# Where the gate products of the heads stand in an attention stage, and one gate step between two kinds of turning

## The chip, the cores and the metric

The kernel runs on one core of a Trainium2 chip. The metric is the time of one execution on the device, in microseconds (us); the kernel before takes 645.65 us, the median of three runs (645.23 to 645.66). One execution was also recorded by the hardware profiler. Names of engines as in the profile: PE is TensorE (matmuls and transposes), PEld its weight loads, ACT ScalarE, DVE VectorE, POOL GpSimd, SP the engine that issues most DMAs. L152 is line 152 of the kernel before; behind line 688 the changed kernel's lines are three higher.

## The reference

One layer of an encoder: attention heads and a gated linear recurrence (LRU) side by side, on 512 tokens of 2048 numbers each.

```python
h = rms_norm(x, norm_w)
proj = jnp.einsum('bsd,de->bse', h, w_in)
q, k, v, g_attn, xr, g_lru = jnp.split(proj, SPLITS, axis=-1)
attn_out = attention_group(q, k, v, q_norm_w, k_norm_w)
lru_out = lru_group(xr, conv_w, conv_b, lru_wa, ...)
mixed = jnp.concatenate([rms_norm(attn_out, attn_norm_w) * jax.nn.silu(g_attn),
                         rms_norm(lru_out, lru_norm_w) * jax.nn.silu(g_lru)], axis=-1)
return x + jnp.einsum('bse,ed->bsd', mixed, w_out)
```

There are 8 query heads and 2 key/value heads of 128; all queries of a head see all 512 keys. `g_attn` and `g_lru` are 1024 columns wide each.

## The kernel before

Every product of fp32 values is made of three matmuls (`mm3`, L152 to L154): both operands are split into a rounded high part and a remainder (`wh`, `wl` of a weight; L224 on ACT rounds, L226 on DVE subtracts), and high by high, high by low and low by high are added up in one PSUM bank. The stages follow each other on PE: the LRU input, keys and values, queries, then **the attention stage** (some 255 to 418 us in the profile), which alone the change touches, then the rest of the gates and the output projection.

In the attention stage two streams are woven on PE by hand; PE's and POOL's order is the program's, while ACT's, DVE's and SP's is set by a scheduler from priorities, ahead of the run, and each engine then works strictly through its own list.

**The chain** is `attention` (from L671). It runs over half heads d = 0 to 18; half head d makes the scores of two of the four 128-query blocks of head d//2, and what earlier half heads left to do. Within a half head the order on PE is: `values` (even d only: 12 matmuls of head (d-4)//2); `turn_weights` twice, the transposes (L639) of two probability blocks of half head d-2, split on ACT and DVE at L581 and L582; at odd d up to 11 `turned`, the transposes (L577) of the queries of head d//2 + 2, split by the same lines; then the two scores S0 and S1 (three matmuls each). Each score is reduced on DVE (L626), scaled on ACT (L627) and exponentiated on ACT (L630, one [128 x 512] pass that is the last to read the bank), its sum inverted on DVE (L631) and the block scaled on POOL (L632).

Everything the chain writes on PE goes to four PSUM banks named `mm` in turn, so the instruction after four others waits until the oldest bank has been read.

**The fill** is `gates` (from L1256), a list of steps. Each step is six [128 x 128] by [128 x 512] matmuls. `weave` takes as many steps from it as the chain yields: four before half head 0, then `STEPS = 1, 3`, one behind S0 and three behind S1. `PLAN` (L1254) is the list of units; a unit is two steps.

- `u` (`gl_units`, L1165): the LRU gate, a [512 x 2048] by [2048 x 1024] product done as **seven products** of half the size in each dimension (named P1, Q6, P2, Q5, Q3, Q7, Q4 in that order; eight steps each), with sums and differences of quarters. All seven accumulate in the same two `pj` banks (first half of the tokens, second half). After the last step of a product `product_done` (L1140) empties the two banks on ACT (P1, L1147) or DVE (L1150 to L1161). The left operand of P1, P2 and Q4 is x itself, that of the others is a sum read back from DRAM and split at L1180 and L1181 (`dh`, `dl`).
- `G` (`ga_units`, L1197): a chunk of the gate of heads 0 and 1, 256 input columns of the eight, accumulating over all eight chunks in the other two `pj` banks. One [128 x 512] tile holds a chunk's weights, split at L1208 and L1209.
- `H`: the same for heads 2 and 3, after the others.

Weights arrive through three raw buffers (`wr`), loaded from SP, and four pairs of `wh`, `wl`. At every second step from the fifth on, POOL issues one DMA that builds sums of `w_out` in DRAM (L835, L838).

Of the kernel before, what the change touches and what calls it, by code (L numbers as in the profile page):

```python
# [23 lines left out]
NH = 8  # L24
# [19 lines left out]
STEPS = 1, 3  # L44
# [18 lines left out]
def hybrid_kernel(  # L63
# [540 lines left out]
    def turned(rot, h, by=SOON):  # L604

        q = b4(F32R)
        soon(split_ps, turn(rot, h), q[:, 0, :], q[:, 1, :], by=by)
        return q[:, 0, :], q[:, 1, :]

    def weights(q, g, t, r, by):  # L610

        qh, ql = q
        tt = slice(t * P, (t + 1) * P)
        sc = mm()
        mm3(sc, qh[:, tt], ql[:, tt], kth[g], ktl[g], True, True)
        return soon(softmax, sc, r, by=by)
# [18 lines left out]
    def turn_weights(p, t, pth, ptl):  # L635
        tt = slice(t * P, (t + 1) * P)
        pt = mm()
        for s in range(NT):
            nc.tensor.transpose(pt[:, s * P : (s + 1) * P], p[:, s * P : (s + 1) * P], ident)  # L639
        p3 = pt.rearrange("p (s q) -> p s q", q=P)  # L640
        soon(split_ps, p3, pth[:, :, tt], ptl[:, :, tt])

    def values(h, pth, ptl):

        gs = slice(h // G * HD, (h // G + 1) * HD)
        o = mm()
        for s in range(NT):
            mm3(o, vh[s][:, gs], vl[s][:, gs], pth[:, s, :], ptl[:, s, :], s == 0, s == NT - 1)
        if h % 2 == 0:
            ap_[h // 2] = aring.tile([P, 2, SEQ], F32, name=nm("av"))  # L650
        av, asum = ap_[h // 2][:, h % 2, :], sums["a"]
        nc.scalar.copy(av, o)
        if h == 0:
            nc.scalar.activation(asum, av, AF.Square)
        else:
            sq = k2()
            nc.scalar.activation(sq, av, AF.Square)
            nc.gpsimd.tensor_add(asum, asum, sq)

    def turned_weights():  # L660
        return [
            pools["low"].tile([P, NT, SEQ], F32R, tag="pt", bufs=ATT_PT, name=nm("pt"))
            for _ in range(2)
        ]
# [6 lines left out]
    def attention(rots):  # L671

        pts, ps_ = {0: turned_weights()}, {}
        qs = {h: turned(rots[0], h, FIRST) for h in range(2)}
        yield 4
        for d in range(2 * NH + 3):
            h, half = divmod(d - 4, 2)
            if h >= 0 and half == 0:
                values(h, *pts.pop(h))
            h, half = divmod(d - 2, 2)  # L680
            if 0 <= h < NH:
                if half == 0:
                    pts[h] = pts.get(h) or turned_weights()
                for t in (2 * half, 2 * half + 1):
                    turn_weights(ps_.pop((h, t)), t, *pts[h])
            h, half = divmod(d, 2)
            if h < NH:
                if half == 1 and h + 2 < NH:
                    qs[h + 2] = turned(rots[(h + 2) // G], (h + 2) % G)
                for e, t in enumerate((2 * half, 2 * half + 1)):  # L690
                    r = q_r[NT * (h // G) + t][:, h % G : h % G + 1]
                    ps_[h, t] = weights(qs[h], h // G, t, r, SOON if d else FIRST)
                    yield STEPS[e]
            elif d < 2 * NH + 2:
                yield 2
            else:
                yield 0
# [360 lines left out]
    for step in proj_feat(C_XR, a1, first, given):  # L1058
# [8 lines left out]
        c, e = step  # L1067
# [153 lines left out]
    def lru_gates(j):  # L1221

        tiles = [halves_of[n, s] for n in (("c", "d"), ("b", "a"))[j] for s in range(2)]
        for t, tile_ in enumerate(tiles):
            nc.scalar.activation(tile_, tile_, AF.Silu, scale=rstd[:, t : t + 1])
        yield
        for t, tile_ in enumerate(tiles):
            nc.scalar.activation(tile_, tile_, AF.Identity, scale=r_lru[0][:, t : t + 1])
        yield
        for m in range(4):  # L1230
            pt = mm()
            for t, tile_ in enumerate(tiles):
                nc.tensor.transpose(  # L1233
                    pt[:, t * P : (t + 1) * P], tile_[:, m * P : (m + 1) * P], ident
                )
            dst = hp[2 * j + m // 2][:, m % 2, :]
            nc.vector.scalar_tensor_tensor(
                dst, dst, v1(R_LN + 4 * j + m), pt, op0=ALU.mult, op1=ALU.mult
            )
            yield  # L1240

    def heads_gates(res):

        for g in res:
            nc.scalar.activation(g, g, AF.Silu)
        yield
        for e, g in enumerate(res):
            dst = ap_[0][:, e, :]
            nc.vector.scalar_tensor_tensor(
                dst, dst, v1(R_AN + e), g, op0=ALU.mult, op1=ALU.mult  # L1250
            )
            yield

    PLAN = "GGGuuuu" "uuuu" "uuuuG" "uuuuG" "uuGuuG" "uuuuG" "uuuu" "HHHHHHHH"  # L1254

    def gates():  # L1256
        early, b = [], [pj() for _ in range(4)]
        units = {"u": gl_units(b[:2]), "G": ga_units(0, early, b[2:]), "H": ga_units(1, late, b[2:])}
        todo = iter(())
        for n, unit in enumerate(itertools.chain.from_iterable((u, u) for u in PLAN)):  # L1260
            done = next(units[unit])
            if n >= 4 and n % 2 == 0:
                next(out_sums, None)
            if done == "Q4":
                todo = itertools.chain(todo, lru_gates(1))
            elif unit == "G" and len(early) == 2 and n == PLAN.rindex("G") * 2 + 1:
                todo = itertools.chain(lru_gates(0), heads_gates(early))
# [5 lines left out]
    with tc.manual_schedule(engines={mybir.EngineType.Pool}):  # L1273
        weave(fill, attention(rots))
        for _ in range(8):
            next(fill)
# [107 lines left out]
```

## Time and profile before

| what | value |
|---|---|
| median of three runs | 645.65 us |
| the profiled execution | 644.75 us |
| its span, first to last instruction | 643.0 us |
| PE busy in the span | 637.2 us (99%) |
| 255 to 440 us: PE, DVE, ACT, POOL busy | 183.97, 138.91, 143.61, 69.03 of 185.00 us |
| granted clock of TensorE in that window | 1.00 |

A row of the timeline gives an instruction's start, its duration, engine, line, operation, what it writes and reads, and, in brackets, idle time ahead of it and what ended that. Matmuls overlap: a [128 x 512] one has a duration of 0.39 us while the next starts 0.23 us after it, so "busy" holds short waits too, and the distance between starts is what tells a wait.

### The profile page before, as it was taken

The page shows a single profiled execution, that of the slowest core. Times are in us where ns is not written, and L with a number is a line of the kernel's source. Part 1 is how long each engine was busy: PE and PEld are TensorE (multiplying, and loading weights), DVE is VectorE, ACT ScalarE, POOL GpSimd, SP SyncE. Part 2 cuts the span into 40 slices and gives each one's busy share as a digit, 9 for nine tenths or more (in the row PEclk, how much of TensorE's full clock was granted, in tenths as well). Part 3 has the DMA queues.
Part 4 walks back from the last instruction along what each step waited for, and adds up shares of the span by engine and source line. Part 5 has one row for each costly group of instructions (what it writes and reads, how often), then busy time and mean ns, then how long its engine had stood idle before and what let it go on. Part 6 is the DMA issues. An engine that isn't in the chain of part 4 may idle for free.

```text
span 643.0 us, 8959 instructions
## 1 busy us (share of the span) xinstructions
PE 637.2 (99%) x2962; PEld 527.6 (82%) x2962; DVE 508.3 (79%) x886; ACT 392.2 (61%) x733; POOL 132.4 (21%) x173
## 2 busy tenths in 40 slices
PE   9999999999999999999999999999999999999997
PEld 6888888888888888887888888888888888888886
DVE  5877679996699994977677868749928988699994
ACT  3543799489955524877696897764444654343441
POOL 0003303223051501543343343221000000010000
PEclk9999999999999999999999999999999999999999
DMA  8947977898767555499989977763365857586322
GB/s 294 293 140 207 234 202 161 245 240 200 171 164 226 165 178 168 148 250 269 264 219 260 266 193 193 164 162 102 98 195 192 298 178 245 186 278 213 120 93 98
DMA packets 68782, 128.19 MB, mean 199 GB/s; under 512 B 5504, under 2 KB 24320, under 8 KB 68480
## 3 DMA queue, kind: packets, MB, share of 16 engines
q1 hardware_dynamic: 55856, 90.25, 43.0%
q0 software_dynamic: 12704, 37.23, 25.5%
q8 instruction: 23, 0.38, 0.2%
q14 instruction: 23, 0.19, 0.1%
q10 hardware_dynamic: 176, 0.14, 0.1%
HBM read 119.21 MB, written 41.95 MB: 251 GB/s over the span
## 4 chain that ended last, share of the span: by engine, by line
PE 97%; DVE 1%; ACT 1%; issue 0%
PE pj L152 19%; PE pj L154 19%; PE pj L153 19%; PE mm L989 13%; PE pj L989 11%; PE mm L153 3%; PE mm L152 3%; PE mm L154 3%; PE mm L639 2%; PE mm L256 1%; PE pj L332 1%; PE mm L577 1%; PE mm L1233 1%; PE mm L1028 0%; DVE pt L582 0%; PE mm L722 0%
## 5 line engine op out<-in xcount | busy, mean ns | idle before, releaser
L224 ACT CAST wh<-wr 128x512 fp32r<-128x512 f32 x151 | 90.0, 618 | 60.8 <-PE pj L154 21.1
L226 DVE TENSOR_TENSOR wl<-wr,wh 128x512 fp32r<-128x512 f32 (+1 forms) x153 | 103.8, 701 | 23.9 <-ACT wh L224 22.4
L152 PE MATMUL pj<-x,wh 128*128 128x512 f32 x248 | 97.8, 394 | 0.0
L153 PE MATMUL pj<-x,wh 128*128 128x512 f32 x248 | 96.7, 390 | 0.0
L154 PE MATMUL pj<-x,wl 128*128 128x512 f32 x248 | 96.7, 390 | 0.0
L152 PE MATMUL pj<-wh,x 128*128 128x512 f32 x240 | 94.1, 392 | 0.6 <-DVE ev L1150 0.6
L154 PE MATMUL pj<-wh,x 128*128 128x512 f32 x240 | 93.5, 390 | 0.0
L153 PE MATMUL pj<-wl,x 128*128 128x512 f32 x240 | 93.4, 389 | 0.0
L783 ACT CAST oh<-rw 128x512 fp32r<-128x512 f32 x94 | 56.3, 620 | 38.8 <-PE mm L989 15.5
L784 DVE TENSOR_TENSOR ol<-rw,oh 128x512 fp32r<-128x512 f32 x94 | 61.7, 685 | 10.8 <-ACT oh L783 6.5
L153 PEld LDWEIGHTS pj<-x,wh 128*128 128x128 f32 x248 | 46.6, 188 | 9.8 <-DVE x L259 0.5
L154 PEld LDWEIGHTS pj<-x,wl 128*128 128x128 f32 x248 | 46.5, 188 | 9.7
L152 PEld LDWEIGHTS pj<-x,wh 128*128 128x128 f32 x248 | 46.6, 188 | 9.6
L152 PEld LDWEIGHTS pj<-wh,x 128*128 128x128 f32 x240 | 45.1, 188 | 10.1 <-DVE ev L1150 1.0
L154 PEld LDWEIGHTS pj<-wh,x 128*128 128x128 f32 x240 | 45.0, 188 | 9.5
L153 PEld LDWEIGHTS pj<-wl,x 128*128 128x128 f32 x240 | 45.1, 188 | 9.3
L989 PE MATMUL mm<-ol,mh 128*128 128x512 f32 (+1 forms) x128 | 49.0, 382 | 0.0
L989 PE MATMUL mm<-oh,ml 128*128 128x512 f32 (+1 forms) x128 | 48.9, 382 | 0.0
L989 PE MATMUL mm<-oh,mh 128*128 128x512 f32 (+1 forms) x128 | 48.9, 382 | 0.0
L921 POOL DMA_DIRECT2D out_dram<-xt x12 | 6.5, 541 | 189.5 <-DVE xt L957 139.8
L632 POOL TENSOR_SCALAR k<-k,sm 128x512 f32<-128x512 f32 x32 | 27.7, 866 | 67.7 <-DVE sm L631 56.2
L989 PE MATMUL pj<-oh,mh 128*128 128x512 f32 (+1 forms) x104 | 39.7, 382 | 0.0
(240 smaller groups left out, 1351.3 us busy)
## 6 DMA issues: line engine op xcount, KB each, us to landing
wr<-in_w_in_dram SPq DMA_DIRECT2D x59, 512.0 KB, 4.3
rw<-in_w_out_dram SPq DMA_DIRECT2D x63, 256.0 KB, 3.6
gs<-in_w_in_dram POOLq DMA_DIRECT2D x24, 512.0 KB, 6.6
ts<-in_w_out_dram POOLq DMA_DIRECT2D x24, 512.0 KB, 7.8
wr<-gs SPq DMA_DIRECT2D x16, 512.0 KB, 5.2
rw<-ts SPq DMA_DIRECT2D x31, 256.0 KB, 4.4
wr<-in_w_in_dram SPq DMA_DIRECT2D x17, 256.0 KB, 4.4
gs<-gs POOLq DMA_DIRECT2D x8, 512.0 KB, 7.3
```

Source lines behind the costliest of these rows:

```text
L152: nc.tensor.matmul(acc, lh, rh, start=start, stop=False)
L153: nc.tensor.matmul(acc, lh, rl, start=False, stop=False)
L154: nc.tensor.matmul(acc, ll, rh, start=False, stop=stop)
L224: rounded(hi[:, c], raw[:, k, c])
L226: nc.vector.tensor_sub(lo[:, c], raw[:, k, c], f(hi[:, c]))
L256: nc.tensor.transpose(pt[:, t * P : (t + 1) * P], xc[:, h * n + t, ks], ident)
L632: nc.gpsimd.tensor_scalar(p, p, sm, 0.0, op0=ALU.mult, op1=ALU.add)
L639: nc.tensor.transpose(pt[:, s * P : (s + 1) * P], p[:, s * P : (s + 1) * P], ident)
L783: nc.scalar.copy(hi, src)
L784: nc.vector.tensor_sub(lo, src, f(hi))
L921: (queue or nc.gpsimd).dma_start(of[t * P : (t + 1) * P, os_], xts[g][t][:, cs])
L989: nc.tensor.matmul(bank[key][:, to], lh[:, a, ts_], rh[:, cols], start=i == 0 and j == 0, stop=i == 7 and j == 2,)
```

## The change

Two edits, both on the order of the stage; every computation stays.

In `PLAN` the 36 units `u` and `G` are the same ones, placed otherwise. Before, three chunks `G` stood at the start, none behind P1 and Q6, one behind each of P2, Q5, Q3 and Q7, and one in the middle of Q3. Now two stand at the start and one behind each of the first six products. From the end of Q3 on the list is as before.

In `attention`, at d = 3, 5, 7, 9 and 11, one step is taken between `turn_weights` and `turned`, and one less behind S1, so that a half head still takes four.

```diff
             if h < NH:
-                if half == 1 and h + 2 < NH:
+                turn = half == 1 and h + 2 < NH
+                if turn:
+                    if d > 1:
+                        yield 1
                     qs[h + 2] = turned(rots[(h + 2) // G], (h + 2) % G)
                 for e, t in enumerate((2 * half, 2 * half + 1)):
                     r = q_r[NT * (h // G) + t][:, h % G : h % G + 1]
                     ps_[h, t] = weights(qs[h], h // G, t, r, SOON if d else FIRST)
-                    yield STEPS[e]
+                    yield STEPS[e] - (e and turn and d > 1)
...
-    PLAN = "GGGuuuu" "uuuu" "uuuuG" "uuuuG" "uuGuuG" "uuuuG" "uuuu" "HHHHHHHH"
+    PLAN = "GGuuuuG" "uuuuG" "uuuuG" "uuuuG" "uuuuG" "uuuuG" "uuuu" "HHHHHHHH"
```

Three places show how the instructions move.

PE, where P1 ends and Q6 begins (banks `pj_524`, `pj_525` are those of the seven products, `pj_526`, `pj_527` those of `G`). Before:

```order
L152 MATMUL pj_525_2637<-wh_579_2852,x2_120_526 128x512
L153 MATMUL pj_525_2637<-wl_580_2853,x2_120_526 128x512
L154 MATMUL pj_525_2637<-wh_579_2852,x2_121_527 128x512
L152 MATMUL pj_524_2636<-wh_590_2892,dh_588_2888 128x512
L153 MATMUL pj_524_2636<-wl_591_2893,dh_588_2888 128x512
L154 MATMUL pj_524_2636<-wh_590_2892,dl_589_2889 128x512
```

Now:

```order
L152 MATMUL pj_527_2639<-x2_73_305,wh_581_2856 128x512
L153 MATMUL pj_527_2639<-x2_74_306,wh_581_2856 128x512
L154 MATMUL pj_527_2639<-x2_73_305,wl_582_2857 128x512
L152 MATMUL pj_524_2636<-wh_590_2892,dh_588_2888 128x512
L153 MATMUL pj_524_2636<-wl_591_2893,dh_588_2888 128x512
L154 MATMUL pj_524_2636<-wh_590_2892,dl_589_2889 128x512
```

Directly ahead of Q6's first matmul stood P1's last; now the second of two steps of `G` stands there, and P1's last step is ahead of the half head's transposes and its two scores.

DVE in half head 9: `pt` is the split of the two turned probability blocks (it empties the banks mm_749 and mm_750 before, mm_743 and mm_744 now), the `ev` rows empty the two product banks behind Q5, `b4` is the split of turned queries. Before:

```order
L1155 TENSOR_TENSOR ev_747_3535<-pj_524_2636,ev_641_3099 128x512
L226 TENSOR_TENSOR wl_770_3616<-wr_764_3604,wh_769_3615 128x512
L1155 TENSOR_TENSOR ev_748_3537<-pj_525_2637,ev_642_3101 128x512
L1181 TENSOR_TENSOR dl_783_3681<-draw_517_2615,dh_782_3680 128x512
L226 TENSOR_TENSOR wl_785_3685<-wr_781_3677,wh_784_3684 128x512
L582 TENSOR_TENSOR pt_722_3440<-mm_749_3539,pt_721_3439 128x4x128
L582 TENSOR_TENSOR pt_722_3440<-mm_750_3546,pt_721_3439 128x4x128
L582 TENSOR_TENSOR b4_751_3553<-mm_752_3554,b4_751_3553 128x512
```

Now:

```order
L1184 TENSOR_TENSOR dl_779_3672<-draw_516_2614,dh_778_3671 128x512
L226 TENSOR_TENSOR wl_781_3676<-wr_777_3668,wh_780_3675 128x512
L582 TENSOR_TENSOR pt_718_3431<-mm_743_3526,pt_717_3430 128x4x128
L582 TENSOR_TENSOR pt_718_3431<-mm_744_3533,pt_717_3430 128x4x128
L226 TENSOR_TENSOR wl_783_3680<-wr_777_3668,wh_782_3679 128x512
L582 TENSOR_TENSOR b4_752_3562<-mm_753_3563,b4_752_3562 128x512
L1158 TENSOR_TENSOR ev_758_3588<-pj_524_2636,ev_641_3099 128x512
L1158 TENSOR_TENSOR ev_759_3590<-pj_525_2637,ev_642_3101 128x512
```

The two `pt` rows, which stood behind the emptying of Q5's banks and a pair of splits, now stand ahead of it.

ACT in half head 7: `pt` is the split of turned probabilities, `b4` that of queries, the `ev` rows are the LRU gate's Silu and scaling of a finished quarter (L1225 and L1228 before, L1228 and L1231 now), the rows with `k2` the exponentials of S0 and S1. Before, up to the exponential of S1:

```order
L1228 ACTIVATE ev_585_2881<-ev_585_2881,r_l_2365 128x512
L224 CAST wh_732_3474<-wr_729_3467 128x512
L1228 ACTIVATE ev_586_2883<-ev_586_2883,r_l_2365 128x512
L627 ACTIVATE mx_697_3345<-mx_697_3345,q_r2_94 128x1
L1180 CAST dh_730_3470<-draw_516_2614 128x512
L224 CAST wh_734_3478<-wr_729_3467 128x512
L630 ACT_TABLE_LOAD
L630 ACTIVATE k2_698_3348,sm_699_3349<-mm_696_3341,mx_697_3345,q_r2_94 128x512
...
L627 ACTIVATE mx_708_3379<-mx_708_3379,q_r3_95 128x1
L630 ACTIVATE k2_709_3382,sm_710_3383<-mm_707_3375,mx_708_3379,q_r3_95 128x512
```

Now:

```order
L1228 ACTIVATE ev_572_2824<-ev_572_2824,rstd_104 128x512
L581 CAST b4_697_3346<-mm_698_3347 128x512
L1228 ACTIVATE ev_573_2826<-ev_573_2826,rstd_104 128x512
L627 ACTIVATE mx_700_3358<-mx_700_3358,q_r2_94 128x1
L224 CAST wh_730_3469<-wr_725_3458 128x512
L630 ACT_TABLE_LOAD
L630 ACTIVATE k2_701_3361,sm_702_3362<-mm_699_3354,mx_700_3358,q_r2_94 128x512
L224 CAST wh_739_3505<-wr_736_3498 128x512
L627 ACTIVATE mx_704_3376<-mx_704_3376,q_r3_95 128x1
L1183 CAST dh_737_3501<-draw_516_2614 128x512
L224 CAST wh_741_3509<-wr_736_3498 128x512
L630 ACTIVATE k2_705_3379,sm_706_3380<-mm_703_3372,mx_704_3376,q_r3_95 128x512
```

Between the query split and the exponential of S1 there are two scalings (L1228 before) fewer; they now follow that exponential. The Silu pair and its table load (one row above those shown), of which the table load and the first Silu stood ahead of the two `pt` splits, now stand behind both.

## The prediction

> **What bounds the kernel now.** I read the page's first and fourth parts, then the wait list of PE for the stage that the change touches, then the timeline of PE at each wait, and last ACT's and DVE's timeline at the places that get less room. The page says that PE is the bound and the chain of waits is PE itself:
>
> ```profile
> PE 637.2 (99%) x2962; PEld 527.6 (82%) x2962; DVE 508.3 (79%) x886; ACT 392.2 (61%) x733; POOL 132.4 (21%) x173
> PE 97%; DVE 1%; ACT 1%; issue 0%
> ```
>
> So a change that only reorders can gain what PE waits, and nothing else: all matmuls stay. The list of PE's waits between 255 and 440 us (engine, line, waited for: us in total, times, longest) seems to leave under a microsecond:
>
> ```profile
> PE pj L152 <- DVE ev L1150: 0.6, 1, 0.6
> PE pj L152 <- ACT ev L1147: 0.2, 1, 0.2
> ```
>
> But a matmul's duration reaches 0.16 us past the start of the next, and hides that much of any wait. The starts tell it whole. PE's timeline in four places of the stage:
>
> ```profile
> 279.54 0.39 PE L154 MATMUL pj<-wh,x 128*128 128x512 f32 x1
> 280.18 0.50 PE L152 MATMUL pj<-wh,dh 128*128 128x512 f32 x1 [0.24 <-ACT ev L1147]
> 280.51 0.39 PE L153 MATMUL pj<-wl,dh 128*128 128x512 f32 x1
> ...
> 297.54 0.39 PE L152 MATMUL pj<-wh,dh 128*128 128x512 f32 x1
> ...
> 298.68 0.39 PE L154 MATMUL pj<-wh,dl 128*128 128x512 f32 x1
> 299.67 0.50 PE L152 MATMUL pj<-wh,x 128*128 128x512 f32 x1 [0.60 <-DVE ev L1150]
> 300.00 0.40 PE L153 MATMUL pj<-wl,x 128*128 128x512 f32 x1
> ...
> 342.90 0.40 PE L154 MATMUL pj<-x,wl 128*128 128x512 f32 x1
> 343.36 0.50 PE L152 MATMUL mm<-kt,b 128*128 128x512 f32 x1
> 343.69 0.40 PE L153 MATMUL mm<-kt,b 128*128 128x512 f32 x1
> ...
> 415.04 0.39 PE L152 MATMUL mm<-pt,v 128*128 128x512 f32 x1
> 415.55 0.50 PE L153 MATMUL mm<-pt,v 128*128 128x512 f32 x1
> 415.89 0.40 PE L154 MATMUL mm<-pt,v 128*128 128x512 f32 x1
> ```
>
> From 297.54 to 298.68 there are five starts: 0.228 us each, so a step of six takes 1.37. Against that, with the late start behind the wait counted too (0.33 where 0.23 is usual):
> - first matmul of Q6 (280.18): 0.64 - 0.23 = 0.41, and 0.10 behind it: **0.51**;
> - first of P2 (299.67): 0.99 - 0.23 = 0.76, and 0.10: **0.86**;
> - S1 of half head 9 (343.36): 0.46 - 0.23 = 0.23, and 0.10: **0.33**;
> - the last head's values (415.04): 0.51 - 0.23 = 0.28, and 0.11: **0.39**.
>
> I went through the starts from 255 to 440 us and found no other over 0.1 us that is not the plain change from transposes to matmuls. The four are 2.09 us: that is all the change can win.
>
> **What they wait for.** The brackets name it at 280.18 and 299.67; the chain of waits has the row ahead of 280.18, and those ahead of 343.36 (start, us, what):
>
> ```profile
> 279.65 0.48 ACT ev L1147
> ...
> 340.82 0.68 DVE ev L1155
> 341.50 0.60 DVE dl L1181
> 342.10 0.60 DVE wl L226
> 342.70 0.61 DVE pt L582
> ```
>
> At the first two it is the product banks: the next product begins directly behind the one before, and ACT or DVE has to empty the banks first. At 343.36 it is an `mm` bank: S1 takes the bank of the first turned probability block, whose split (`pt`, L582) stood in DVE's list behind the emptying of Q5's banks, a `dl` and a `wl`. The fourth (the values) lies where neither PE's nor the other engines' order changes.
>
> **The change part by part.**
>
> *A chunk of G behind P1 and behind Q6.* Two steps, 2.7 us, on the other two banks now stand between the products. From P1's last step to Q6's first there are now eight transposes (0.9 us), two scores (0.7 each) and the two steps, 5 us in all, for two copies of some 0.5 us. From Q6 to P2 it is the two steps and eight transposes, 3.6 us, for two DVE rows of 0.6 us. Both waits go: -0.51 and -0.86. The two chunks came from the start (three to two) and from the middle of Q3. At the start, P1 is now needed one unit, 2.7 us, earlier; its weights' split takes the place in ACT's and DVE's lists that the third chunk had, and SP's list loads them where it loaded that chunk. Until the end of Q3 the units stand at most one unit from where they stood, so I cost the loads at nothing: the list of PE's waits has no DMA in it. POOL's DMA issues keep their order; five of about 1 us each move ahead of one probability scaling. The latest of the scalings in the middle of the stage is that of S1 of half head 7:
>
> ```profile
> 332.96 0.69 POOL L632 TENSOR_SCALAR k<-k,sm 128x512 f32<-128x512 f32 x1 [1.36 <-DVE sm L631]
> ```
>
> It ends at 333.65, and the transposes of half head 9 that need it begin at 339.74 (below): 6.1 us. I cost this at nothing too.
>
> *One step between turned probabilities and turned queries, five times.* It gives the bank of the first block one more step before S1 takes it, and in half head 9 DVE's new list has `pt` ahead of the emptying. The turned blocks are there at 339.74 + 1.03:
>
> ```profile
> 339.74 1.03 PE L639 MATMUL mm<-ident,k 128*128 128x128 f32 x8
> 340.75 1.06 ACT L581 CAST pt<-mm 128x512 fp32r<-128x512 f32 x2
> 339.99 0.90 DVE L226 TENSOR_TENSOR wl<-wr,wh 128x512 fp32r<-128x512 f32 x1
> ```
>
> ACT has a `dh` and a `wh` in front, which wait for the step ahead of the transposes to release their buffers: 339.8 + 1.1, two casts to 342.0, DVE's splits to 342.7 (a DVE row can be stretched, 0.90 here for 0.68, while POOL works). S1 comes at 343.13 + 1.37 = 344.5. The wait goes with 1.8 us to spare: -0.33.
>
> Its price on PE is a second change between transposes and matmuls. The trace has the very pattern where gate transposes are woven in:
>
> ```profile
> 401.74 0.60 PE L1233 MATMUL mm<-ident,ev 128*128 128x128 f32 x4
> ...
> 403.56 0.60 PE L1233 MATMUL mm<-ident,ev 128*128 128x128 f32 x4
> ```
>
> Four transposes and six matmuls take 1.82 us; four at 0.109 (eight from 339.74 to the queries' at 340.61) and 1.37 make 1.80. So 0.02 each, five times: **+0.10**.
>
> *What the same step takes away.* In those half heads only two steps, not three, follow S1, so S1's bank has 1.37 us less until the next half head's S0 takes it. Before, half head 8 was nearest:
>
> ```profile
> 321.14 1.03 PE L639 MATMUL mm<-ident,k 128*128 128x128 f32 x8
> 322.58 1.06 ACT L581 CAST pt<-mm 128x512 fp32r<-128x512 f32 x2
> 324.64 0.72 ACT L1228 ACTIVATE ev<-ev,r_l 128x512 f32<-128x512 f32 x1
> 327.72 1.28 ACT L630 ACT_TABLE_LOAD   x1
> 331.73 0.78 ACT L630 ACTIVATE k<-mm,mx,q_r 128x512 f32<-128x512 f32 x1
> 332.82 0.48 PE L152 MATMUL mm<-kt,b 128*128 128x512 f32 x1
> ```
>
> The last ACT row is the exponential of S1 of half head 7: it ended at 332.51, 0.31 us ahead of S0. With the same list it would now be 1.06 late. But the list is another: from the end of the `pt` casts (323.64) to that exponential's end it took 8.87 us; two scalings leave the stretch (0.72 each with 0.1 of overlap, -1.2), two casts too (0.52 each, -1.0), a Silu and its table load enter (1.28 and 0.6, +1.9): 8.5. And the casts no longer stand behind a table load: the transposes are all done at 321.14 + 1.03, so the second cast, half of the 1.06, ends at about 322.75 rather than 323.64. That makes 331.3, some 1.5 us ahead of S0. I take no wait.
>
> The Trainium skill, page "ScalarE: Activation LUTs", section "What ACT_TABLE_LOAD costs", gives 2.66 us for a switch of tables, a load of about 1.28 and a drain of about 1.38. The load agrees with the row (1.28); a drain does not show, since the exponential of S0 starts 0.02 behind the load's end (329.00):
>
> ```profile
> 329.02 0.78 ACT L630 ACTIVATE k<-mm,mx,q_r 128x512 f32<-128x512 f32 x1
> ```
>
> By the page the two switches in the new stretch would take 2.8 us more, S0 would wait 1.3, and the sum would come out at 645.5.
>
> Half heads 12 and 13 get tighter too. In ACT's new list one `pt` cast of half head 13 (half of a 1.05 pair) stands ahead of the exponential whose bank S1 takes:
>
> ```profile
> 378.57 0.77 ACT L630 ACTIVATE k<-mm,mx,q_r 128x512 f32<-128x512 f32 x1
> 379.33 1.05 ACT L581 CAST pt<-mm 128x512 fp32r<-128x512 f32 x2
> 380.22 0.39 PE L152 MATMUL mm<-kt,b 128*128 128x512 f32 x1
> ```
>
> It ended 0.88 us before S1; less 0.53 leaves 0.35, and a `dh` cast ahead of it that now waits for its buffer may take most of that. From nothing to 0.4 us: I take **+0.10**. In half head 12 the copy of the values' bank falls behind two `pt` casts, about 1.1 us later, with 0.5 us left: 0 to 0.4, I take 0.
>
> *Sum.* -0.51 - 0.86 - 0.33 + 0.10 + 0.10 = **-1.50 us**. The profiled execution took 644.75 us, of which the span is 643.0; it would take 643.25 with a span of 641.5. That execution is 0.9 below the median shown, so the forecast for the median is 645.65 - 1.50 = **644.15 us**, 0.23% faster. About 0.2%, 1.3 us, is what a measurement of this kernel can tell from no change: the forecast lies just past that line.
>
> **The rivals.**
>
> 1. *The even half heads pay.* The cover of S1's bank is too short where ACT is late: half head 8 by 1.06 + 0.10, or half heads 12 and 13 by 0.4 each. For it: 0.31 us was all that was left in half head 8. Against it: the new ACT list above. Net -0.3 to -0.8: 644.9 to 645.3, no change that can be told. Chance 0.25, of which hardly 0.02 for a switch of tables that costs more than its row.
> 2. *The third wait stays, or another of its size comes.* The two at the product boundaries go, nothing else: -1.37 + 0.20 = -1.17, 644.5. For it: DVE is 79% busy and its order is the scheduler's. Chance 0.11.
> 3. *The fourth wait goes as well*, because ACT reaches the tail earlier: -1.9, 643.75. Against it: the lists there are row for row the same, and hang on PE. Chance 0.06.
> 4. *Slower.* The shortened cover decides in every even half head from 4 to 12: the exponential of S1 ends but 0.31 us ahead of where S0 stood, as in half head 7, and S0 now comes 1.37 earlier. Each place then costs 1.06 + 0.10 = 1.16. One is paid by the gain of 1.50 with little left, two leave 645.65 - 1.50 + 2.32 = 646.5, no change that can be told; it decides from the third, 645.65 - 1.50 + 3.48 = 647.6. Against it: that half head had the Silu and its table on ACT. Two half heads later the room was ten times that:
>
> ```profile
> 347.64 0.77 ACT L630 ACTIVATE k<-mm,mx,q_r 128x512 f32<-128x512 f32 x1
> 351.79 0.48 PE L152 MATMUL mm<-kt,b 128*128 128x512 f32 x1
> ```
>
> That is 348.41 against 351.79, 3.4 us, of which 2.0 are left. Chance 0.06.
>
> That the change might not do what it says I leave out: PE's order shows a chunk of G at each of the six boundaries.
>
> **How the numbers follow.** The forecast itself (three waits gone, at most 0.4 us of new ones, so 643.8 to 644.6) gets 0.52; rivals 1 to 4 get 0.25, 0.11, 0.06, 0.06. Faster by over 0.2% means below 644.36: some 0.44 of the forecast's 0.52, rival 3, and 0.04 of rival 2, 0.54 in all. Within 0.2%: the rest of the forecast, rival 1 and most of rival 2, 0.40. Slower: 0.06. The range goes from 643.6 (all four waits gone, or a good set of runs) to 645.3 (rival 1).
>
> **What would show it.** In the changed kernel's profile: no bracket at the first matmul of Q6 and of P2, and starts 0.23 us apart there or right behind a G step; S1 of half head 9 on time; the wait at the last values still 0.39; PE's busy time less by under a microsecond and the span near 641.5. The forecast is wrong if S0 of half head 8 or S1 of half heads 12 or 13 starts late behind an ACT row, or if the first steps of P1 at 261 us wait for weights.

## The result and the profile after

The changed kernel takes **646.56 us** (median of 22 runs, 645.62 to 647.53); the kernel before, on the same chip, 645.47 us (22 runs, 644.81 to 646.35). The ratio is 1.0017, with a 95% interval of 1.0010 to 1.0023: the change is slower by 1.1 us. The forecast was 644.15, with a range from 643.6 to 645.3, 1.50 below a median of 645.65.

The page of the changed kernel has a share of busy PE like that of before, but its chain of waits has DMA in it, where before it was 97% PE. Of these 3%, some 19 us, the weight load below is 8.99 us; another load, of 7.64 us, stands at the kernel's start (3.76 us), far ahead of the stage, and e13 below, the same kernel once more, has 1%:

```profile
PE 638.1 (99%) x2962; PEld 528.0 (82%) x2962; DVE 507.8 (79%) x886; ACT 392.8 (61%) x733; POOL 135.3 (21%) x173
PE 90%; ACT 4%; DMA 3%; DVE 1%; issue 1%; SPq 0%; ACTq 0%
```

The list of PE's waits between 255 and 440 us (line, waited for: us in total, times, longest) has lost both rows of the product banks and has three new ones:

```profile
PE mm L152 <- DVE pt L582: 1.4, 1, 1.4
PE mm L152 <- ACT k L630: 0.5, 1, 0.5
PE mm L1236 <- ACT k L630: 0.2, 1, 0.2
```

PE's timeline shows the places of the prediction: the first matmul of Q6 behind a step of `G`, the first of P2 behind transposes, S1 of half heads 9, 12 and 13, and the last values:

```profile
281.11 0.39 PE L154 MATMUL pj<-x,wl 128*128 128x512 f32 x1
281.34 0.39 PE L152 MATMUL pj<-wh,dh 128*128 128x512 f32 x1
...
303.46 0.48 PE L152 MATMUL pj<-wh,x 128*128 128x512 f32 x1
...
344.41 0.40 PE L154 MATMUL pj<-wh,dl 128*128 128x512 f32 x1
344.64 0.39 PE L152 MATMUL mm<-kt,b 128*128 128x512 f32 x1
...
372.07 0.39 PE L154 MATMUL pj<-x,wl 128*128 128x512 f32 x1
373.82 0.50 PE L152 MATMUL mm<-kt,b 128*128 128x512 f32 x1 [1.36 <-DVE pt L582]
374.16 0.39 PE L153 MATMUL mm<-kt,b 128*128 128x512 f32 x1
...
381.43 0.39 PE L154 MATMUL pj<-wh,dl 128*128 128x512 f32 x1
382.30 0.50 PE L152 MATMUL mm<-kt,b 128*128 128x512 f32 x1 [0.49 <-ACT k L630]
...
417.53 0.39 PE L152 MATMUL mm<-pt,v 128*128 128x512 f32 x1
418.03 0.50 PE L153 MATMUL mm<-pt,v 128*128 128x512 f32 x1
```

The first three waits are gone: 281.11 to 281.34 and 344.41 to 344.64 are the usual 0.23, and 303.46 has no bracket (it is 0.79 behind the start of eight transposes, as the other first matmuls behind eight of them are). The last values still wait, 0.50 from start to start. But S1 of half head 12 starts 1.75 us behind the matmul ahead of it, so it waits 1.52, with the late start behind it (0.34 for 0.23) **1.63**; S1 of half head 13 waits 0.65 and 0.11, **0.76**. Gained are 0.51 + 0.86 + 0.33 = 1.70, lost 2.39 and about 0.26 at gate transposes near 411 us (0.57 from start to start, 0.31 before): a loss of 0.95. From the first step of `G` to the start of the last of the values' matmuls PE took 162.79 us before and 163.71 now, 0.92 more. A second profile of the changed kernel, below, has 1.39 more; the medians differ by 1.09.

Where the two new waits come from stands in the chain of waits, in order of time:

```profile
360.22 0.61 DVE wl L226
...
360.85 8.99 DMA wr<-gs
...
369.92 0.62 ACT wh L224
...
370.55 1.28 ACT L1228
...
371.85 0.72 ACT ev L1228
372.57 0.96 ACT pt L581 x2
...
381.38 0.88 ACT k L630 x2
...
382.30 0.50 PE mm L152
```

A weight load (512 KB of `gs`, for the second of Q7's four units) is issued when DVE has split older weights, and takes 9 us to land. ACT's list has the rounding of these weights (`wh`) ahead of the Silu's table load, and the Silu ahead of the turned probability blocks (`pt`), whose bank S1 of half head 12 takes. ACT's timeline has two waits for DMA there:

```profile
368.50 0.62 ACT L1183 CAST dh<-draw 128x512 fp32r<-128x512 f32 x1 [1.06 <-DMA draw<-ds]
369.92 0.62 ACT L224 CAST wh<-wr 128x512 fp32r<-128x512 f32 x1 [0.79 <-DMA wr<-gs]
370.55 1.28 ACT L1228 ACT_TABLE_LOAD   x1
371.85 0.72 ACT L1228 ACTIVATE ev<-ev,rstd 128x512 f32<-128x512 f32 x1
372.48 1.05 ACT L581 CAST pt<-mm 128x512 fp32r<-128x512 f32 x2
373.42 0.60 ACT L652 COPY av<-mm 128x512 f32<-128x512 f32 x1
```

The same rows in the kernel before, whose first matmul of that half head is at nearly the same time (366.86, now 366.65), have no wait for DMA:

```profile
366.84 0.62 ACT L1180 CAST dh<-draw 128x512 fp32r<-128x512 f32 x1
367.57 0.62 ACT L224 CAST wh<-wr 128x512 fp32r<-128x512 f32 x1
368.21 1.28 ACT L1225 ACT_TABLE_LOAD   x1
...
370.13 0.57 ACT L652 COPY av<-mm 128x512 f32<-128x512 f32 x1
370.60 1.08 ACT L581 CAST pt<-mm 128x512 fp32r<-128x512 f32 x2
```

PE itself uses the late weights only at 380.29, behind the two steps of Q7's first unit (from 376.00 on) and S0 of half head 13. The load was in time for the product, but not for the list that ACT works through.

**Why the loads are late** has two candidates in the trace. The first sum for Q7 (`draw`) is issued by SP seven microseconds later than before. First the kernel before, then the changed one:

```profile
350.12 0.34 SPq L1178 DMA_DIRECT2D draw<-ds  x1
...
357.59 0.32 SPq L1178 DMA_DIRECT2D draw<-ds  x1
...
360.04 3.95 SPq L1172 DMA_DIRECT2D wr<-gs  x2
```

```profile
357.35 0.34 SPq L1181 DMA_DIRECT2D draw<-ds  x1
...
360.25 0.32 SPq L1181 DMA_DIRECT2D draw<-ds  x1
360.85 2.12 SPq L1175 DMA_DIRECT2D wr<-gs  x2
```

The loads that ACT waits for are those of Q7's second unit, and they are issued less late than the first sum: the sum 2.7 us (357.59 and 360.25), the weights 0.8 us (360.04 and 360.85). The rest of their lateness is in the time to landing: 8.99 us for the weights, at most 7.53 before (360.04 to 367.57, where ACT reads them without a wait).

The first sum's buffer comes free when Q3's third sum has been split, and ACT makes that `dh` (at 348.40 before, 355.71 now) as soon as PE has done Q3's first unit and freed a `dh`. Before, this unit ended at 348.3, ahead of half head 10; now, since the chunk of `G` that stood in the middle of Q3 is placed ahead of it, the unit comes after the values and S0 of half head 10 and ends at 355.7. And POOL issues two DMAs of the `w_out` sums back to back, since the extra step puts the second ahead of the scaling of S0. First before, then now:

```profile
359.28 1.06 POOL L835 DMA_DIRECT2D ts<-in_w_out_dram  x1
365.13 0.53 POOL L838 DMA_DIRECT2D ts<-ts  x1
```

```profile
359.15 1.08 POOL L838 DMA_DIRECT2D ts<-in_w_out_dram  x1
359.75 1.00 POOL L841 DMA_DIRECT2D ts<-ts  x1
```

### The profile page after: what moved, and what is told of

Same layout as the page of the kernel before. It is cut to its first block, busy times and chain, and to the rows that moved or that the text cites. A ratio compares the mean times of both kernels' runs of the same rounds, so it can differ in the third digit from the quotient of the medians.

```text
span 645.4 us, 8955 instructions
## 1 busy us (share of the span) xinstructions
PE 638.1 (99%) x2962; PEld 528.0 (82%) x2962; DVE 507.8 (79%) x886; ACT 392.8 (61%) x733; POOL 135.3 (21%) x173
## 3 DMA queue, kind: packets, MB, share of 16 engines
q1 hardware_dynamic: 55856, 90.25, 42.5%
q0 software_dynamic: 12704, 37.23, 25.2%
## 4 chain that ended last, share of the span: by engine, by line
PE 90%; ACT 4%; DMA 3%; DVE 1%; issue 1%; SPq 0%; ACTq 0%
PE pj L152 18%; PE pj L153 18%; PE pj L154 18%; PE mm L992 13%; PE pj L992 11%; PE mm L153 3%; PE mm L152 3%; PE mm L154 3%; PE mm L639 1%; DMA wr<-gs 1%; DMA wr<-in_w_in_dram 1%; ACT wh L224 1%; PE mm L256 1%; PE mm L577 1%; ACT k L630 1%
```

## The experiments

The theories, as the expectations name them. LOADS (later LEAD): the new `PLAN` has Q7's loads issued too late. SUMS (later CROWD): the moved sums run beside them. STEP: the extra step shortens what covers the banks at half heads 12 and 13, loads or no loads. "ACT waits" below is what ACT waited for DMA in the 10 us or so ahead of the Silu's table load. "Lateness" is the start of that table load minus the start on PE of the turning of half head 12's probabilities: in the changed kernel 370.55 - 369.37 = +1.18, before 368.21 - 369.59 = -1.38. The waits are worked out from PE's starts as above, and the four columns ahead of the median are of one profiled execution each. Times and ratios are against the kernel before in the same set of runs; its median was 645.22 to 645.47 us in the four sets.

| kernel | ACT waits | lateness | S1, half head 12 | S1, half head 13 | median, us | ratio (95%) |
|---|---|---|---|---|---|---|
| before | 0 | -1.38 | 0 | 0 | 645.47 | |
| changed | 2.01 | +1.18 | 1.63 | 0.76 | 646.56 | 1.0017 (1.0010 to 1.0023) |
| e13, changed again | 2.65 | +1.80 | 2.25 | 0.73 | 646.66 | 1.0017 (1.0008 to 1.0026) |
| e1, PLAN alone | 0.71 | -0.16 | 0 | 0.58 | 644.33 | 0.9988 (0.9976 to 1.0000) |
| e2, step alone | 0.16 | -0.80 | 0 | 0.44 | 645.51 | 1.0001 (0.9992 to 1.0010) |
| e3, two loads left out | 0 | -0.76 | 0 | 0.48 | 643.97 | 0.9975 (0.9965 to 0.9984) |
| e5, sums as before | 2.45 | +0.22 | 0.67 | 0.77 | 645.52 | 1.0001 (0.9993 to 1.0010) |
| e4, G in mid Q3 | 0 | -1.06 | 0 | 0.18 | 643.79 | 0.9978 (0.9968 to 0.9987) |
| e6, e4 without the step | 1.00 | -0.49 | 0 | 0.26 | 644.48 | 0.9985 (0.9976 to 0.9994) |
| e8, sums two turns later | 0 | -1.05 | 0 | 0.18 | 643.98 | 0.9979 (0.9970 to 0.9988) |
| e9, PLAN alone, sums later | 0 | -1.07 | 0 | 0 | 644.26 | 0.9982 (0.9973 to 0.9990) |
| e10, e4 and e8 | 0 | -1.06 | 0 | 0.18 | 643.75 | 0.9976 (0.9963 to 0.9988) |
| e11, no step at d = 11 | 1.27 | +0.29 | 0 | 0.96 | 644.41 | 0.9984 (0.9975 to 0.9993) |
| e12, sums one turn later | 0.75 | -0.08 | 0.37 | 0.74 | 644.97 | 0.9989 (0.9980 to 0.9998) |

**e1, the new PLAN alone.** The attention of the kernel before:

```diff
-                    if d > 1:
-                        yield 1
...
-                    yield STEPS[e] - (e and turn and d > 1)
+                    yield STEPS[e]
```

> The new PLAN alone; attention as before. Three theories for the change's 1.63 us wait at S1 of half head 12 and 0.76 us at S1 of half head 13. LOADS: taking the chunk G out of the middle of Q3 lets Q7's loads be issued some 7 us later, ACT waits for them (1.06 and 0.79 us in the changed kernel) ahead of the Silu and the turned blocks. Then this kernel has the two product boundaries free (-1.37) but ACT still waits over 1 us for Q7's second unit, S1 of half head 12 is over 0.8 us late, and the time is 645.0 to 645.8. SUMS: the extra step moves POOL's DMAs of the sums ahead of a scaling, so that they run beside Q7's loads. Then ACT waits less than 0.3 us here and the time is 644.0 to 644.5. STEP: the extra step takes the cover from the even half heads whatever the loads do. Then no wait over 0.3 us at half heads 12 and 13 and 644.0 to 644.5. The third wait (S1 of half head 9) should be back where the old attention order stands.

Measured: 644.33 against 645.44 us. ACT waits 0.71 us, less than LOADS alone wanted; half head 12 has no wait, half head 13 has 0.58. The third wait of before, at S1 of half head 9, does not come back. So the plan alone does not lose, though its gain is hardly told (the interval reaches 1.0000), and it alone does not make the loads late enough.

**e2, the extra step alone.** The PLAN of the kernel before:

```diff
-    PLAN = "GGuuuuG" "uuuuG" "uuuuG" "uuuuG" "uuuuG" "uuuuG" "uuuu" "HHHHHHHH"
+    PLAN = "GGGuuuu" "uuuu" "uuuuG" "uuuuG" "uuGuuG" "uuuuG" "uuuu" "HHHHHHHH"
```

> The extra step alone; PLAN as before, so that a chunk G stands in the middle of Q3 and Q7's loads can be issued as early as before. LOADS: ACT does not wait for Q7's loads (under 0.3 us), half head 12 has no wait over 0.3; the two boundary waits (0.51, 0.86) stay, the third (0.33) goes, 645.2 to 645.6. SUMS: POOL's DMAs stand as in the changed kernel, so ACT waits over 1 us for loads and half head 12 pays over 1 us: 646.2 to 647. STEP: half heads 12 and 13 pay 0.4 or more each, without ACT waiting for a load: 646 to 647.

Measured: 645.51 against 645.44 us, as LOADS wanted it: ACT waits 0.16 us and half head 12 nothing, though POOL's two DMAs stand together as in the changed kernel. The third wait is gone, half head 13 pays 0.44. SUMS alone falls. Alone the parts give -1.1 and 0.1 us, together +1.1: the loss is made by both at once.

**e3, the two loads left out.**

```diff
+                    keep = name == "Q7" and c == 1
-                    raw = pools["wr"].tile([P, 2, SEQ], F32, tag="wr", bufs=3, name=nm("wr"))
-                    nc.sync.dma_start(
-                        raw, gsum[c][right] if isinstance(right, int) else two_gl(c, *right)
-                    )
+                    if not keep:
+                        raw = pools["wr"].tile([P, 2, SEQ], F32, tag="wr", bufs=3, name=nm("wr"))
+                        nc.sync.dma_start(
+                            raw, gsum[c][right] if isinstance(right, int) else two_gl(c, *right)
+                        )
...
-                        nc.sync.dma_start(draw, dsum[c][:, left])
+                        if not keep:
+                            nc.sync.dma_start(draw, dsum[c][:, left])
```

> The changed kernel without the two loads of Q7's second unit (its weights and its x sums are split again from what the buffers hold; the LRU gate's product Q7 is so computed from other numbers, every instruction on PE, ACT and DVE stays). LOADS: ACT has no wait for DMA between 365 and 371 us, S1 of half head 12 is at most 0.3 us late, S1 of half head 13 at most 0.5, and the time falls by 1.5 to 2.2 against the changed kernel, to 644.3 to 645.0. SUMS: the same here (the loads are what is late in both). STEP: the waits stay at 1 us or more together, 645.8 to 646.6.

Measured: 643.97 us, 2.6 below the changed kernel and more than was expected. The wait at half head 12 is gone, 0.48 are left at half head 13. Every instruction of PE, ACT and DVE is still there, so what cost the time is the landing of two loads, and STEP falls as the main cause.

**e5, the five sums DMAs behind the scaling of S0 again.**

```diff
+    held = []
...
+                        held.append(0)
                         yield 1
...
                     ps_[h, t] = weights(qs[h], h // G, t, r, SOON if d else FIRST)
+                    if held and held.pop():
+                        next(out_sums, None)
...
-                next(out_sums, None)
+                if held:
+                    held[0] = 1
+                else:
+                    next(out_sums, None)
```

> The changed kernel, but POOL issues the five DMAs of the sums that the extra step had moved behind the scaling of S0 again, as in the kernel before. LOADS: Q7's loads are issued as late as in the changed kernel; ACT still waits over 1 us for the second unit's, half head 12 still pays 1 us or more: 646.1 to 646.8. SUMS: the loads land 1.5 to 2 us earlier, ACT's wait falls below 0.5 us, half head 12 pays under 0.4: 644.6 to 645.3. STEP: no change, 646.2 to 646.8.

Measured: 645.52, between the theories. The two DMAs are apart again, but another, issued at 360.14, still stands beside the loads, and it is Q7's first unit that is late now, on ACT's timeline:

```profile
363.25 0.62 ACT L1188 CAST dh<-draw 128x512 fp32r<-128x512 f32 x1 [1.96 <-DMA draw<-ds]
364.36 0.62 ACT L224 CAST wh<-wr 128x512 fp32r<-128x512 f32 x1 [0.49 <-DMA wr<-gs]
```

ACT makes some of it up before the table load: lateness +0.22, half head 12 waits 0.67. S0 of half head 10 waits here too, 0.40 us, which the table does not hold: it starts at 350.75, 1.16 behind the start of the transposes where 0.79 is usual, and the chain of waits has the exponential of S1 of half head 9 ahead of it. Moving the sums a little moves the wait to other loads.

**e4 and e6, a chunk of G in the middle of Q3 again,** taken from the two at the start; all six boundaries keep theirs. e4 has the extra step, e6 has not:

```diff
-    PLAN = "GGuuuuG" "uuuuG" "uuuuG" "uuuuG" "uuuuG" "uuuuG" "uuuu" "HHHHHHHH"
+    PLAN = "GuuuuG" "uuuuG" "uuuuG" "uuuuG" "uuGuuG" "uuuuG" "uuuu" "HHHHHHHH"
```

> The changed kernel with a chunk G put back into the middle of Q3, taken from the two at the start; a chunk still stands behind each of the first six products, and the extra step stays. LEAD (Q7's loads are issued too late because Q3's first unit is done a unit later): the first sum of Q7 is issued some 7 us earlier again, ACT waits for loads under 0.3 us, half head 12 has no wait and half head 13 about the 0.44 of the kernel with the step alone; the boundary waits are gone. Time 643.8 to 644.6. CROWD (POOL's two sums beside the loads are what makes them late): they stand as in the changed kernel, so half head 12 still pays over 0.6 and the time is 644.9 to 646. A wait for weights at the start of P1, which is needed a unit earlier still, would show as a row of PE with a DMA in it near 259 us.

> The same PLAN (one chunk G at the start, one behind each of six products, one in the middle of Q3) with the attention of the kernel before, without the extra step. Both LEAD and CROWD: ACT waits for loads under 0.2 us; no wait at the product boundaries, at half head 9 or 12, at half head 13 under 0.3. All but the last of the four waits of before are gone: -1.70, 643.6 to 644.2, the fastest. If it is not below the 644.33 of the new PLAN alone, the loads' lateness there (ACT 0.71 us) cost nothing that the middle chunk gives back.

Measured: e4 643.79 against 645.22 us. The first sum of Q7 is issued at 349.12 and ACT waits for no load, with the sums where the changed kernel has them: here lead alone is a remedy. e6, expected to be the fastest, takes 644.48. Without the step the third wait is back (0.34 at half head 9), ACT waits 1.00 us for one of Q7's weight loads, and S1 of half head 3 waits 0.78 for a `pt` split that DVE's list has behind a `wl`, a `dl` and a `wl` (283.62 to 286.37). Q7's loads are issued as early as in the kernel before (sums at 350.00 and 357.46, weights at 359.91), POOL's sums stand as there, and still ACT waits, where that kernel did not: e6's profile is of the slowest of its eleven executions (645.18), and no run here says why the load was late in it. So an early issue isn't a sure remedy. By the medians the step is worth more than it costs with this PLAN, but the intervals of e4 and e6 overlap.

**e8 and e9, the sums two turns (four steps) later,** in the changed kernel (e8) and with the new PLAN alone (e9):

```diff
-    def sums_in_dram(sum_, two):
+    def sums_in_dram(sum_, two, order=SUMS):
...
-        for step in SUMS.split():
+        for step in order.split():
...
-    late, halves_of, out_sums = [], {}, sums_in_dram(tsum, two_out)
+    late, halves_of, out_sums = [], {}, sums_in_dram(
+        tsum, two_out, SUMS.replace("aA3 pC2", "-- -- aA3 pC2")
+    )
```

> The changed kernel with the two sums DMAs that run beside Q7's first loads (and all behind them) issued two turns, four steps, later. Q7's loads are issued as late as in the changed kernel. LEAD alone: ACT still waits over 1.2 us before the Silu's table load, half head 12 still pays over 0.8: 645.6 to 646.5. CROWD alone: ACT waits under 0.3 us, half head 12 nothing: 644.5 to 645.0. Both together (as the runs with the one or the other taken back suggest): ACT waits 0.3 to 1 us, half head 12 pays 0 to 0.6: 644.8 to 645.5.

> The new PLAN alone (no extra step) with the same two sums DMAs issued two turns later. In the run of the new PLAN alone ACT waited 0.71 us for Q7's second unit, S1 of half head 13 was 0.58 us late and the gate transposes near 408 us 0.7. If ACT's lateness by the loads is what half head 13 pays for, its wait falls below 0.2 here and the time is 643.6 to 644.1; if not, it stays at 0.4 to 0.6 and the time is that of the new PLAN alone, 644.1 to 644.6. The moved sums may collide with loads of the next products: then a new DMA wait shows on ACT behind 372 us.

Measured: e8 643.98, better than "both together" had it, with the waits gone as "CROWD alone" wanted: Q7's loads are issued as late as in the changed kernel (360.25 there, 359.21 here, where the stage began 1.04 us earlier), but ACT waits for none, and PE's waits at half head 12 are gone. e8's rows of ACT for the second unit:

```profile
366.12 0.61 ACT L1185 CAST dh<-draw 128x512 fp32r<-128x512 f32 x1
366.63 0.62 ACT L224 CAST wh<-wr 128x512 fp32r<-128x512 f32 x1
367.27 1.28 ACT L1230 ACT_TABLE_LOAD   x1
```

What moved is the load on the DMA engines. In the stretches of five microseconds (the last two columns are the DMA engines' share and GB/s) the changed kernel has them full from 360 to 370 us:

```profile
360.00:365.00 5.00, 5.00 (x25) 4.12 (x24) 4.86 (x9) 3.19 (x8) 0.76 (x2) 1.00 1.02 278
365.00:370.00 5.00, 5.00 (x26) 4.17 (x26) 4.00 (x7) 3.05 (x8) 0.69 (x1) 1.00 1.04 373
```

and in e8 they have room from 365 us on:

```profile
360.00:365.00 5.00, 5.00 (x25) 4.13 (x24) 4.75 (x9) 3.72 (x9) 0.05 (x1) 1.00 0.95 355
365.00:370.00 5.00, 5.00 (x28) 4.23 (x27) 3.76 (x7) 4.88 (x10) 1.80 (x3) 1.00 0.64 218
```

Full DMA engines alone don't make the wait: in the kernel before they are as full (1.01 and 1.06), but there the loads of Q7's first unit had been issued earlier (the sum at 350.12, now 357.35; the weights at 355.51, now 358.11).

The Trainium skill, page "DMA: Bandwidth & Descriptors", section "Issuing engines are not separate DMA queues", says that DMAs started by different engines run on the same 16 DMA engines and interleave. These runs agree: DMAs that POOL issued made those late that SP issued (the second unit's weights took 8.99 us to land in the changed kernel, and at most 6.82 in e8, 359.81 to 366.63). e9 shows that half head 13's wait in e1 was the same lateness: it is 0 here. No new wait for DMA shows on ACT from 372 to 413 us. The time, however, can't be told from e1's: 0.96 us below the kernel before, for 1.11 there, and above the 643.6 to 644.1 that were expected. 0.41 us are left at the gate transposes.

**e10, both remedies together.** The diffs of e4 and e8.

> The changed kernel with both remedies: a chunk G back in the middle of Q3 (taken from the start) and the two sums DMAs issued two turns later. Each alone took the waits at half heads 12 and 13 away (643.79 and 643.98). If the late loads were the whole loss, nothing is left to gain: no DMA wait on ACT, 643.6 to 644.1. If each remedy left a part, 643.2 to 643.6.

Measured: 643.75 against 645.43 us. Nothing beyond either remedy can be told, as the late loads had it as the whole loss; a few tenths more would be hidden in the interval.

**e11, no extra step at d = 11:**

```diff
-                    if d > 1:
+                    if 1 < d < 11:
...
-                    yield STEPS[e] - (e and turn and d > 1)
+                    yield STEPS[e] - (e and turn and 1 < d < 11)
```

> The changed kernel with the extra step at d = 3, 5, 7, 9 only, not at d = 11. Only there do the sums DMAs meet Q7's loads, and there the order of POOL is then that of the kernel before. Late loads as the cause: ACT waits about 0.7 us as in the run of the new PLAN alone, half head 12 has no wait, half head 13 up to 0.6, 644.2 to 644.8. If the steps at the other places cost too (cover in even half heads, order of the sums), 645 or more.

Measured: 644.41, as the late loads had it, though ACT's wait (1.27, for about 0.7) and half head 13's (0.96, for up to 0.6) are longer than was expected. Of the five steps only the last does harm that can be told. ACT is even later than in e5 (+0.29), but half head 12 does not wait: in e11's list, as in e1's and that of before, the copy of the values' bank stands ahead of the two `pt` casts, and S1 takes that bank (it starts at 371.17, and DVE begins the split of the first turned block only at 371.52).

**e12, the sums one turn later,** as e8 with one `--`.

> The changed kernel with the sums DMAs issued one turn later instead of two: one of the two still runs beside Q7's first loads. If the time that the loads lose grows with the sums that run beside them, it lies between the changed kernel (ACT waits 2.0 us, half head 12 pays 1.63) and the run with two turns (no wait): ACT 0.5 to 1.5, half head 12 0.2 to 1.0, 644.4 to 645.6. If one is enough to make them as late: as the changed kernel, 646 to 646.8. If one has room: no wait, 643.8 to 644.3.

Measured: 644.97, in between, as "the time that the loads lose grows with the sums" has it. ACT waits 0.21 us for the second unit's sum and 0.54 for its weights, half head 12 pays 0.37.

**e13, the changed kernel again.** No edit.

> The changed kernel once more, beside these three on one chip. Late loads as the cause: the wait at half head 12 is again over 1 us and stands behind a DMA wait of ACT, half head 13 0.4 to 0.9, 646.0 to 646.8. The start of the stage, 256.73 us in the first profile against 255.16 in that of before, though the code ahead of it is the same but for two weight loads, should come out between 255.1 and 256.0 as in the other runs; if it is at 256.7 again, the change costs time ahead of the stage as well.

Measured: 646.66 us, a ratio of 1.0017 once more. ACT's two waits for the second unit's loads are longer in this execution, 1.38 for the sum (367.39) and 1.27 for the weights (369.29), and half head 12 pays 2.25. The stage begins at 255.49: the 256.73 of the first profile was that one execution.

**The sums fit one rule.** In the kernels with the step at d = 11 the two waits together are the lateness + 1.2: 2.39 at +1.18, 2.98 at +1.80, 1.44 at +0.22, 1.11 at -0.08, 0.44 at -0.80, 0.48 at -0.76, 0.18 at -1.05; none is off by more than 0.05. Without it they are the lateness + 0.7: 0.96 at +0.29, 0.58 at -0.16, 0.26 at -0.49, none at -1.07. What ACT is late by beyond that room PE waits, microsecond for microsecond. The 0.5 between the two is one `pt` cast: with the step ACT's list has it ahead of the exponential whose bank S1 of half head 13 takes (in the changed kernel 380.91, the exponential at 381.38), without it both casts come behind (in e11 the exponential at 378.87, the casts at 379.63).

## Why the prediction was wrong

**Right.** The reading of the four waits: three go and the fourth stays, 0.38 for 0.39. The sign that the prediction named for its own failure, a late S1 at half heads 12 and 13, came as well. The price of the second change between transposes and matmuls: from the turned probabilities (339.87 in the changed kernel) to the queries' S0 (342.47) it is 2.60, for 1.22 and a step of 1.37 before, so 0.01, for 0.02 forecast. The even half head 8: the exponential of S1 of half head 7 ends at 330.70 + 0.78 = 331.48, for 331.3 forecast, and S0 is on time at 332.96. And at a switch of tables the load takes 1.28 us (370.55), the cast ahead of it ends at 370.54 and the Silu begins 0.02 behind it. By the figure of the Trainium skill, page "ScalarE: Activation LUTs", section "What ACT_TABLE_LOAD costs", a drain of 1.38 would come with it; this trace does not show one. And the sum: with the loads in time, e8's stage on PE is 161.23 us for 162.79 before, -1.56 for -1.50, and e4, e8 and e10 are 1.43, 1.24 and 1.68 us faster than before.

**The step that failed** is "I cost the loads at nothing: the list of PE's waits has no DMA in it". In place of nothing the runs show some 2.2 us: 2.39 at half heads 12 and 13, of which 0.18 are left with the loads in time (e8). Three things were wrong in the step.

- PE was the wrong engine to ask. Q7's weights were in time for PE by some 9 us even when late (split by 371.3, used at 380.29); ACT's list has them ahead of work for PE that is due. Before, ACT rounded them at 367.57 with its table load 1.38 ahead of the turning, a room of which nothing in the prediction spoke. ACT's own list in the kernel before had a wait for a weight load in it, at a place where no wait of PE came of it:

```profile
312.08 0.62 ACT L224 CAST wh<-wr 128x512 fp32r<-128x512 f32 x1 [1.87 <-DMA wr<-gs]
```

- "At most one unit from where they stood" is true of the units, but a load is issued when a buffer comes free, and the buffer when PE has done an earlier unit. Moved by one unit, Q3's first unit crossed the values and S0 of half head 10 and ended 7.4 us later (348.3, 355.7), and Q7's first sum was issued 7.2 later, the second unit's 2.7.
- "POOL's DMA issues keep their order; five of about 1 us each move ahead of one probability scaling" looked at the scaling alone. What counts is where the DMAs run: one was issued 5.4 us earlier (365.13, 359.75), into Q7's loads.

**Half head 12**, taken at 0 with an upper end of 0.4, is 1.63. The mechanism written there was another: the copy of the values' bank behind two `pt` casts. S1 takes the bank of the first turned block instead (the bracket names the split of it; the copy ends at 374.02, behind S1's start). So the four `mm` banks aren't always taken strictly in turn, as the description of the kernel has it. Of **half head 13** place and releaser were right, an exponential behind one `pt` cast: 0.18 with the loads in time, for 0.10 forecast, and 0.76 with ACT late. Rival 1 had both places at 0.4 each and left no room for more; its price was bounded by ACT's list without a wait in it. Rival 4, the slower one, needed three even half heads to pay through S0's bank; none did in the changed kernel, and one in e5. That the two parts are harmless apart and harmful together was in no rival.

**Still open**: the 0.26 us at the gate transposes near 411 us, and 0.41 at the same place in e9. They wait for an exponential, and no run here changes them alone. The late loads aren't their cause: e10, where ACT waits for none, has 0.27 there. Open too is why e6's load, issued as early as before, came 1.00 us late.

## What to carry to other kernels

When work is moved, follow each load from the instruction that frees its buffer to the first engine that touches its data, and look at what stands behind that touch in this engine's list: an engine that works strictly through a list turns a load that is early enough for the matmuls into a wait for something else. Put the times of all DMA issues, of every queue, beside each other in the new order; a DMA issue that costs its engine nothing still takes the DMA engines from the others. And test two parts of a change apart and together: here each is harmless, both cost, and together with the step, the plan with the middle chunk kept, or the sums moved by two turns, gives about what was forecast.

## What the runs showed of the hardware

By the times of their packets, a byte of the sums takes the DMA engines longer than a byte of a plain load. The DMA queues' rows from 354 to 371 us (packets, MB, share of 16 engines; `q0` is POOL's, since it alone shrinks in e8), first the changed kernel, then e8:

```profile
q0 software_dynamic: 713, 2.08, 55.9%
q1 hardware_dynamic: 892, 2.45, 38.1%
```

```profile
q1 hardware_dynamic: 1152, 3.15, 52.4%
q0 software_dynamic: 346, 0.91, 24.2%
```

That is 27% of the stretch for a MB on `q0` in both (55.9 / 2.08 and 24.2 / 0.91), against 16 and 17% on `q1`: 1.6 to 1.7 times as much. In the kernel before it is 1.4 times in the same stretch (54.4% for 2.08 MB, 46.1% for 2.48 MB), and 1.4 over the whole run of the changed kernel (25.2% for 37.23 MB, 42.5% for 90.25 MB). A packet's time may hold waiting behind others. Many of POOL's add to what stands in DRAM, and some only copy, so which of the two is dear isn't told apart here. The median time to landing of a 256 KB `draw` in that stretch fell from 6.0 to 3.8 us in e8; the first three of the four are issued at the same distance from the start of the stage, the fourth 0.8 us earlier.
